# Seven-product block matmuls in another order, sums in place, three convolution tiles, a later norm product

## The chip, the cores and the metric

One core of a Trainium2 chip runs the kernel. The metric is the device time of one execution in microseconds (us). The median of 3 timed runs of the kernel before is 1835.4 us (1834.36 to 1836.99). TensorE (PE) does matmuls into PSUM, VectorE (DVE), ScalarE (ACT) and GpSimd (POOL) do elementwise work, SyncE (SP) issues the DMA transfers.

## The reference, cut to what matters

One layer of a hybrid decoder on x of 1024 tokens by 1024 channels, in float32:

```python
h = rms_norm(x, g_pre)
proj = h @ w_in            # q,k,v,z_a | u,v_s,z_s | z_m, xBC, dt | 3 x 1024 gates
y_att = sliding_window_attention(q, k, v, sinks, rel_bias) * silu(z_a)
y_sg  = chunked_spatial_gate(u, v_s, ...) * silu(z_s)       # u * (tril(W) LN(v_s) + b)
y_ssm = ssd_mixer(z_m, xbc, dt, ...)   # conv of 4 taps + silu on xbc, chunked scan over 8 chunks
                                       # x 4 groups, * silu(z_m), RMS norm per group
merged = sum(sigmoid(gate_i) * (y_i @ w_br_i))              # three branches
out = x + rms_norm(merged @ w_out, g_post)
```

## The kernel before, in words

Each float32 operand of a big matmul is split into a high and a low part (`hi`, `lo`), and three matmuls (hi*hi, hi*lo, lo*hi) stand for one product. The order of TensorE's instructions is written out by hand in the whole kernel; in the pair stage (below), up to its last chunk, that of the other engines and of SP's queue is too. Every engine works its own instructions strictly in that order.

**Stages.** Input norm and first projections (to 350 us), attention with more projections beside it (to 429), then the **pair stage** (429 to 1365), then the three branch matmuls and the output matmul (1365 to the end).

**The pair stage.** 39 units are done, each one projection of 256 output columns (a pair of 128) by 1024 tokens and 1024 channels, as a 2 by 2 block matmul with seven block products in place of eight (class `PairStream`, line 197). The blocks of h are `hB[half of tokens, half of channels]`; three sums of them (`s1`, `s2`, `s4`) are made once. A unit's weights come in two `raw` tiles (3 buffers in turn): the first holds blocks B11 and B12, the second B21 and B22. Four sums of weight blocks, T1 to T4, are made per unit by POOL (`_sum`, line 227), the first in place of B12, the other three in `ts` tiles, of which there are two. `_prepare(q)` (line 236) does the loads and sums for product q and makes its `hi` (ACT, line 257) and, one product later, its `lo` (DVE, line 232). It runs four products ahead of TensorE. The sums therefore stand in POOL's queue between other work, and a sum whose tile is still being read waits, with all that is behind it.

`_step` (line 273) issues one product: 12 matmuls of 128 by 512 columns (lines 293 to 295) into a PSUM tile, of which four are in turn; then `_work()`; then the evacuation, in which ACT or DVE adds the product to running sums in `tp` tiles (lines 309 to 317). A product of a unit is named i = 0 to 6 here. When a block of the result is complete, `evac` gets it: blocks 22, 12, 21, 11 at i = 3, 4, 5, 6.

`_work` (line 264) advances the follow-up jobs by one step per product. At most two jobs are active, as they share two `acc` tiles. A convolution job (`conv`, line 748; the blocks of x, B and C, in units called x units) takes five steps: ACT scales (line 752), DVE does two taps and one tap (line 755), ACT tanh (lines 760, 761), POOL multiplies (line 763) and SP stores. A z job takes two steps (ACT lines 713 and 714, POOL line 716 and a store), a gate job one. The units run as x z x z x g, then three times x z x z x g g, then eight zu units (z of the spatial gate with u) and four g.

**The chunk work** of the scan (`chunk`, line 874) runs beside the products: 32 chunks, one begun every six products (every five in the last group of eight), each advanced by a step per product. Step 0 transposes on TensorE into two PSUM tiles `ps_tr` (lines 884 to 888), which DVE and ACT empty (lines 890, 894 and ACT's `btok`, line 892). Step 4 has DVE's `t1` (line 932), which empties the PSUM tile that the matmuls of step 6 (line 952) use next. Step 13 (12 in the last group) is the **norm product** (line 974), one matmul into `ps_tr`. There are two `ps_tr` tiles; the norm product takes the one that the transposes of the second next chunk used last, and those were issued at step 12 (10 in the last group), so it waits for `btok`.

After the chunks, the spatial gate (lines 1004 to 1062) does eight groups between the remaining products: a load `vg`, POOL (line 1025), DVE (line 1026), TensorE (lines 1035, 1040), DVE. The last four products stand behind it. Then the branch matmuls read their inputs `y` into tiles that lie where those of the pair stage were.

Of the kernel before, what the change touches and what calls it, by code (L numbers as in the profile page):

```python
# [11 lines left out]
F32 = mybir.dt.float32  # L12
F32R = mybir.dt.float32r
AF = mybir.ActivationFunctionType
ALU = mybir.AluOpType
# [4 lines left out]
P = 128  # L20
S = 1024
# [6 lines left out]
NPY = 2  # L28
# [12 lines left out]
def hybrid_kernel(ctx, tc, t, out):  # L41
    nc = tc.nc
    V, A, G, T = nc.vector, nc.scalar, nc.gpsimd, nc.tensor
# [10 lines left out]
    def psum(pool, tag):  # L54
        return pool.tile([P, 512], F32, name="ps_" + tag, tag=tag)
# [141 lines left out]
    class PairStream:  # L197
# [17 lines left out]
                b = self.b.setdefault(u, {})  # L215
                b[f"B{k + 1}1"], b[f"B{k + 1}2"] = r[:, 0:512], r[:, 512:]

        def _sum(self, u, out, x, y, op):
            b = self.b.get(u, {})
            if out in b or u >= len(self.units):  # L220
                return
            if out == "T1":

                b[out] = b[x]
            else:
                b[out] = self.pool.tile([P, 512], F32, name="ts", bufs=2)
            G.tensor_tensor(b[out], b[x], b[y], op=op)  # L227

        def _second(self):
            if self.late is not None:  # L230
# [4 lines left out]
        def _prepare(self, q):  # L235

            u, i = divmod(q, 7)
            self._second()
            if i == 0:
                for k in range(2):  # L240
                    self._load(u, k)
                self._sum(u, "T3", "B22", "B12", ALU.subtract)
                self._sum(u, "T2", "T3", "B11", ALU.add)
            elif i == 1:
                self._sum(u, "T1", "B12", "B11", ALU.subtract)
                self._load(u + 1, 0)
            elif i == 3:
                self._load(u + 1, 1)
            elif i == 4:
                self._sum(u, "T4", "T2", "B21", ALU.subtract)  # L250
            elif i == 6:
                self._sum(u + 1, "T3", "B22", "B12", ALU.subtract)
            src = self.b[u][("B11", "T2", "T1", "T3", "B22", "T4", "B21")[i]]
            if q % 2 == 0:
                self.slot = [wp.tile([P, 1024], F32R, name=n, tag=n, bufs=3) for n in ("whi", "wlo")]
            hi, lo = (x[:, q % 2 * 512:q % 2 * 512 + 512] for x in self.slot)
            A.copy(hi, src)  # L257
            self.late = lo, src, hi
            self.ops[q] = hi, lo
            if i == 6:  # L260
                del self.b[u]

        def _work(self):

            self.waiting, self.fresh = self.waiting + self.fresh, []
            for _ in range(2 if len(self.waiting) > 3 else 1):
                while self.waiting and len(self.active) < 2 and (len(self.begun) < 2 or self.begun[-2] not in self.active):
                    self.active.append(self.waiting.pop(0))
                    self.begun.append(self.active[-1])
                for job in list(self.active):  # L270
                    if next(job, None) is None:
                        self.active.remove(job)

        def _step(self):
            n = 7 * len(self.units)
            if self.done >= n:
                return None
            while self.prepared < min(n, self.done + 1 + self.AHEAD):
                self._prepare(self.prepared)
                self.prepared += 1  # L280
            if self.prepared == self.done + 1:
                self._second()
            u, i = divmod(self.done, 7)
            hi, lo = self.ops.pop(self.done)
            o = psum(ps_ax, "ax") if self.done % 4 == 3 else psum(ps_mm, "mm")
            self.done += 1
            if i == 0:
                self.t = {}
            t = self.t
            for kt in range(4):  # L290
                ks = slice(kt * P, (kt + 1) * P)
                h0, h1 = (self.lhs(i, part, kt) for part in range(2))
                T.matmul(o, lhsT=hi[:, ks], rhs=h0, start=kt == 0, stop=False)  # L293
                T.matmul(o, lhsT=hi[:, ks], rhs=h1, start=False, stop=False)  # L294
                T.matmul(o, lhsT=lo[:, ks], rhs=h0, start=False, stop=kt == 3)  # L295

            def tmp(name):

                t[name] = self.pool.tile([P, 516], F32, name="tp", bufs=8)
                return t[name][:, 4:]  # L300

            def block(b, name, op=ALU.add):
                d = t[name][:, 4:]
                V.tensor_tensor(d, d, o, op=op)  # L304
                self.units[u][1](b, t[name])

            self._work()
            if i == 0:
                A.copy(tmp("s1"), o)
            elif i == 1:  # L310
                t["u2"] = self.pool.tile([P, 512], F32, name="tu", bufs=1)
                V.tensor_tensor(t["u2"], t["s1"][:, 4:], o, op=ALU.add)
            elif i == 2:
                V.tensor_tensor(tmp("u4"), t["u2"], o, op=ALU.add)
            elif i == 3:
                V.tensor_tensor(tmp("c22"), t["u4"][:, 4:], o, op=ALU.add)
                V.tensor_tensor(tmp("u3"), t["u2"], o, op=ALU.add)
                self.units[u][1](22, t["c22"])
            elif i == 4:
                block(12, "u4")  # L320
            elif i == 5:
                block(21, "u3", ALU.subtract)
            else:
                block(11, "s1")
            return 2.8

        def run(self, n):
# [45 lines left out]
    if True:  # L373

        with tc.tile_pool(name="xp", bufs=1) as xp:
# [96 lines left out]
            n = NB * 32  # L472
# [206 lines left out]
    sop = es7.enter_context(tc.tile_pool(name="sop", bufs=1, side="right", reuse_waits="tile"))  # L679
    s2, s1, s4 = ([sop.tile([P, 4, 512], F32R, name=f"S{i}{part}") for part in range(2)] for i in (2, 1, 4))  # L680

    blocks = [hB[0, 0], s2, s1, hB[1, 0], s4, hB[1, 1], hB[0, 1]]

    ep = es7.enter_context(tc.tile_pool(name="ep", bufs=1, side="right", reuse_waits="tile"))
    pst = PairStream(ep, lambda i, part, kt: blocks[i][part][:, kt, :])
# [6 lines left out]
    def gate_pair(n):  # L692
        def tanh(b, d):
            A.activation(d, d, AF.Tanh, scale=0.5)
            i, half = NGATE + 2 * n + b % 10 - 1, b // 10 - 1
            nc.sync.dma_start(out=gate_dr[i, :, half * 512:(half + 1) * 512], in_=d)
            yield from ()

        def evac(b, d):
            pst.fresh.append(tanh(b, d[:, 4:]))  # L700
        return [t["w_gp"][n][k] for k in range(2)], evac

# [6 lines left out]

    def z_pair(g, n):  # L710
        def silu(b, d):
            th = ap.tile([P, 512], F32, name="acc", bufs=2)
            A.activation(th, d, AF.Tanh, scale=0.5)
            A.activation(th, th, AF.Identity, bias=one)
            yield 1
            G.tensor_tensor(d, th, d, op=ALU.mult)
            store(z_dr, g, b // 10 - 1, 2 * n + b % 10 - 1, d)

        def evac(b, d):
            pst.fresh.append(silu(b, d[:, 4:]))  # L720
        return [t["w_zm"][2 * g + n][k] for k in range(2)], evac

    def zu_pair(g):
        us = {}

        def silu(half, d, u):
            th = ap.tile([P, 512], F32, name="acc", bufs=2)
            A.activation(th, d, AF.Tanh, scale=0.5)
            yield 1
            V.scalar_tensor_tensor(d, th, 1.0, d, op0=ALU.add, op1=ALU.mult)  # L730
            yield 1
            V.scalar_tensor_tensor(d, u, 0.5, d, op0=ALU.mult, op1=ALU.mult)
            nc.sync.dma_start(out=uz_dr[g, :, half * 512:(half + 1) * 512], in_=d)

        def evac(b, d):

            half, d = b // 10 - 1, d[:, 4:]
            if b in (12, 22):
                us[half] = d
            else:  # L740
                pst.fresh.append(silu(half, d, us.pop(half)))
        return [t["w_zu"][g][k] for k in range(2)], evac

    def conv_pair(g, n):

        held = {}

        def conv(half, k, d):
            ti = g * 4 + 2 * n + k if n < 2 else 16 + 4 * k + g
            body = d[:, 4:]  # L750
            acc = ap.tile([P, 512], F32, name="acc", bufs=2)
            A.activation(acc, body, AF.Identity, scale=wcv[:, ti, 3:4], bias=bcv[:, ti:ti + 1])  # L752
            yield 1
            for tap in range(3):
# [11 lines left out]
            else:  # L766
                store(bc_dr, g, half, k, body)

        def evac(b, d):
            half, k = b // 10 - 1, b % 10 - 1  # L770
            if half == 1:
                held[k] = d
                return
            V.memset(d[:, 1:4], 0.0)
            d1 = held.pop(k)
            V.tensor_copy(d1[:, 1:4], d[:, 513:516])
            pst.fresh += [conv(0, k, d), conv(1, k, d1)]

        return [t["w_xbc"][3 * g + n][k] for k in range(2)], evac

# [49 lines left out]
    with tc.tile_pool(name="mp", bufs=1, reuse_waits="tile") as mp, tc.manual_schedule(  # L830
# [43 lines left out]
        def chunk(n):  # L874
# [95 lines left out]
            yield  # L970
            yield
            yield
            pn = psum(ps_tr, "tr")
            T.matmul(pn[:, 0:1], lhsT=ss, rhs=one, start=True, stop=True)
            A.copy(ssum[:, n:n + 1], pn[:, 0:1])
# [91 lines left out]
    spare = {}  # L1067
# [68 lines left out]
    for n in (9, 10, 11):  # L1136
        spare[n] = slot(n)
    pz.tile([P, 384], F32, name="pz_pad")
    for n in (2, 3):
        raws[n] = raw_tile(n)  # L1140
    for n in range(NPY, 9):
        spare[n] = slot(n)
    merged.extend(pz.tile([P, S], F32, name=f"mg{i}") for i in range(8))
    for n in range(NPY, 8):
        ys[n] = load_y(n)
    for un in range(4):
# [128 lines left out]
```

## Time and profile before

| what | us |
|---|---|
| median of 3 runs | 1835.4 |
| the profiled execution: its own time, its span | 1831.66, 1830.0 |
| TensorE busy | 1750.5 (96%) |
| VectorE busy | 1287.7 (70%) |
| ScalarE busy | 844.2 (46%) |
| GpSimd busy | 850.8 (46%) |
| DMA | 243.28 MB, mean 133 GB/s |

A matmul's busy time counts its passage through the array too, so TensorE shows as busy where it merely goes from one matmul to the next; what it loses shows as gaps (the table of waits) and as stretches in which the granted clock is half. A wait is put down to whatever came last.

### The profile page before, as it was taken

The numbers are of one execution on the slowest core, as the hardware profiler recorded it, in microseconds if no ns is written. First come the engines' busy times: TensorE is split into PE (matmuls) and PEld (weight loads), VectorE is DVE, ScalarE is ACT, GpSimd is POOL, SyncE is SP. The second block draws the span as 40 slices with busy tenths as digits, with TensorE's granted clock in tenths as the row PEclk, the third lists the DMA queues.
The fourth block names the chain that finished last, engine by engine and source line by source line (L and its number), as shares of the span: only waits on it lengthen the run. The fifth ranks groups of instructions, "written<-read, shape, count | busy, mean of one in ns | idle before, by whom it ended". The sixth has DMA issues, their size and how long they took to land. (4 is left out here: it accounts for less than half of the span.)

```text
span 1830.0 us, 25921 instructions
## 1 busy us (share of the span) xinstructions
PE 1750.5 (96%) x9181; PEld 1474.7 (81%) x9181; DVE 1287.7 (70%) x1781; ACT 844.2 (46%) x1883; POOL 850.8 (46%) x761
## 2 busy tenths in 40 slices
PE   7999999998999989998999899999988999999998
PEld 6988888897887777877777778887776888888898
DVE  5466667758888888898889878987885284444424
ACT  5245555534555766576666666552233122111221
POOL 1015666665655877587667766667424050000000
PEclk9999999999999999999999999999998999999999
DMA  7221111122334546454644555544767353533204
GB/s 227 67 73 47 47 58 47 58 67 73 115 93 150 173 138 205 126 155 150 202 139 144 155 190 161 157 147 126 236 233 261 127 195 106 181 121 98 81 24 162
DMA packets 165377, 243.28 MB, mean 133 GB/s; under 512 B 13152, under 2 KB 105600, under 8 KB 165120
## 3 DMA queue, kind: packets, MB, share of 16 engines
q1 hardware_dynamic: 165248, 241.63, 41.6%
q8 instruction: 73, 1.20, 0.3%
q14 instruction: 56, 0.46, 0.1%
HBM read 177.99 MB, written 63.59 MB: 132 GB/s over the span
## 5 line engine op out<-in xcount | busy, mean ns | idle before, releaser
L116 PE MATMUL ps_mm<-y,whi 128*128 128x512 f32 x512 | 200.4, 391 | 9.7 <-ACT y L1094 9.7
L117 PE MATMUL ps_mm<-y,whi 128*128 128x512 f32 x512 | 200.3, 391 | 1.4 <-DVE y L1095 1.4
L293 PE MATMUL ps_mm<-h,whi 128*128 128x512 f32 x468 | 194.1, 415 | 7.4 <-ACT vst L354 3.4
L118 PE MATMUL ps_mm<-y,wlo 128*128 128x512 f32 x512 | 199.9, 390 | 0.0
L227 POOL TENSOR_TENSOR ts<-ts,raw 128x512 f32<-128x512 f32 x78 | 123.6, 1585 | 152.9 <-DVE wlo L232 150.3
L98 ACT CAST whi<-raw 128x1024 fp32r<-128x1024 f32 (+1 forms) x69 | 71.5, 1038 | 251.6 <-PE ps_mm L117 224.4
L294 PE MATMUL ps_mm<-h,whi 128*128 128x512 f32 x468 | 185.4, 396 | 0.0
L295 PE MATMUL ps_mm<-h,wlo 128*128 128x512 f32 x468 | 185.2, 396 | 0.0
L232 DVE TENSOR_TENSOR wlo<-raw,whi 128x512 fp32r<-128x512 f32 x156 | 176.4, 1131 | 8.6 <-ACT whi L257 8.4
L89 POOL TENSOR_TENSOR rso<-rso,mhalf_row 128x1 f32<-128x1 f32 x8 | 4.4, 553 | 323.1 <-DVE rso L88 323.1
L755 DVE SCALAR_TENSOR_TENSOR acc<-tp,wcv,acc 128x512 f32<-128x512 f32 x144 | 146.7, 1046 | 2.5 <-ACT acc L752 0.8
L293 PE MATMUL ps_mm<-S,whi 128*128 128x512 f32 x352 | 143.8, 408 | 0.3 <-DVE tp L304 0.3
L295 PE MATMUL ps_mm<-S,wlo 128*128 128x512 f32 x352 | 137.7, 391 | 0.6 <-DVE wlo L232 0.6
L294 PE MATMUL ps_mm<-S,whi 128*128 128x512 f32 x352 | 137.6, 391 | 0.0
L116 PE MATMUL ps_mm<-h,whi 128*128 128x512 f32 x304 | 121.0, 398 | 2.0 <-ACT vst L354 2.0
L257 ACT CAST whi<-raw 128x512 fp32r<-128x512 f32 x156 | 94.6, 612 | 60.9 <-POOL raw L227 45.9
L116 PEld LDWEIGHTS ps_mm<-y,whi 128*128 128x128 f32 x512 | 96.6, 189 | 30.6 <-ACT y L1094 10.5
L1118 DVE SCALAR_TENSOR_TENSOR tm<-gld,ps_mm 128x512 f32<-128x512 f32 x48 | 32.9, 686 | 122.3 <-PE ps_mm L118 122.3
L118 PE MATMUL ps_mm<-h,wlo 128*128 128x512 f32 x304 | 118.6, 390 | 0.0
L117 PE MATMUL ps_mm<-h,whi 128*128 128x512 f32 x304 | 118.6, 390 | 0.0
L117 PEld LDWEIGHTS ps_mm<-y,whi 128*128 128x128 f32 x512 | 96.6, 189 | 22.8 <-DVE y L1095 3.0
L293 PEld LDWEIGHTS ps_mm<-h,whi 128*128 128x128 f32 x468 | 89.7, 192 | 29.6 <-issue 4.1
(242 smaller groups left out, 4945.1 us busy)
## 6 DMA issues: line engine op xcount, KB each, us to landing
seg<-acs_dr SPq DMA_DIRECT2D x64, 256.0 KB, 3.9
raw<-in_w_br_dram SPq DMA_DIRECT2D x32, 512.0 KB, 4.5
yraw<-y_dr SPq DMA_DIRECT2D x32, 512.0 KB, 5.0
gld<-gate_dr SPq DMA_DIRECT2D x32, 512.0 KB, 3.5
raw<-in_w_xbc_dram SPq DMA_DIRECT2D x24, 512.0 KB, 4.0
raw<-in_w_gp_dram SPq DMA_DIRECT2D x22, 512.0 KB, 4.3
gate_dr<-tp SPq DMA_DIRECT2D x44, 256.0 KB, 3.3
raw<-in_w_zm_dram SPq DMA_DIRECT2D x16, 512.0 KB, 3.6
```

The costliest lines, as they stand in the source:

```text
L98: A.copy(hi, raw)
L116: T.matmul(ps, lhsT=whi[:, ks], rhs=rhs(0, kt, half), start=kt == 0, stop=False)
L117: T.matmul(ps, lhsT=whi[:, ks], rhs=rhs(1, kt, half), start=False, stop=False)
L118: T.matmul(ps, lhsT=wlo[:, ks], rhs=rhs(0, kt, half), start=False, stop=kt == KT - 1)
L227: G.tensor_tensor(b[out], b[x], b[y], op=op)
L232: V.tensor_tensor(lo, src, hi.bitcast(F32), op=ALU.subtract)
L257: A.copy(hi, src)
L293: T.matmul(o, lhsT=hi[:, ks], rhs=h0, start=kt == 0, stop=False)
L294: T.matmul(o, lhsT=hi[:, ks], rhs=h1, start=False, stop=False)
L295: T.matmul(o, lhsT=lo[:, ks], rhs=h0, start=False, stop=kt == 3)
L755: V.scalar_tensor_tensor(acc, d[:, 1 + tap:513 + tap], wcv[:, ti, tap:tap + 1], acc, op0=ALU.mult, op1=ALU.add)
L1118: V.scalar_tensor_tensor(tm, gt[0][:, fs], 1.0, ps, op0=ALU.add, op1=ALU.mult)
```

## The change

- The seven products of a unit stand in another order: B11, B21, T2, T1, T3, B22, T4 (before: B11, T2, T1, T3, B22, T4, B21). Blocks 11, 12, 22, 21 are complete at i = 1, 5, 5, 6, so four follow-up jobs come at those. The running sums are made in fewer tiles: `tu` goes, and sums are updated in place. Per unit there are, as before, one ACT copy and seven DVE adds, four `tp` tiles and two small copies of the convolution's edge.
- T2 is written in place of B11 and T3 in place of B12, T1 and T4 in the two `ts` tiles. All four are subtractions. T2 and T3 are issued at `_prepare` step 1, T1 at step 0, T4 at step 4. The next unit's weights are loaded at steps 3 and 5 (before: 1 and 3).
- Three `acc` tiles and up to three active jobs.
- The norm product stands two products later (chunk step 15, in the last group 14).
- The tiles of the branch stage lie in another order over those of the pair stage.

```diff
@@ -215,16 +215,12 @@
...
-        def _sum(self, u, out, x, y, op):
-            b = self.b.get(u, {})
-            if out in b or u >= len(self.units):
+        def _sum(self, u, out, x, y, place=None):
+            if u >= len(self.units) or out in self.b[u]:
                 return
-            if out == "T1":
-
-                b[out] = b[x]
-            else:
-                b[out] = self.pool.tile([P, 512], F32, name="ts", bufs=2)
-            G.tensor_tensor(b[out], b[x], b[y], op=op)
+            b = self.b[u]
+            b[out] = b[place] if place else self.pool.tile([P, 512], F32, name="ts", bufs=2)
+            G.tensor_tensor(b[out], b[x], b[y], op=ALU.subtract)
@@ -239,18 +235,18 @@
...
                     self._load(u, k)
-                self._sum(u, "T3", "B22", "B12", ALU.subtract)
-                self._sum(u, "T2", "T3", "B11", ALU.add)
+                self._sum(u, "T1", "B12", "B11")
             elif i == 1:
-                self._sum(u, "T1", "B12", "B11", ALU.subtract)
+
+                self._sum(u, "T2", "B22", "T1", "B11")
+                self._sum(u, "T3", "B22", "B12", "B12")
+            elif i == 3:
                 self._load(u + 1, 0)
-            elif i == 3:
+            elif i == 4:
+                self._sum(u, "T4", "T2", "B21")
+            elif i == 5:
                 self._load(u + 1, 1)
-            elif i == 4:
-                self._sum(u, "T4", "T2", "B21", ALU.subtract)
-            elif i == 6:
-                self._sum(u + 1, "T3", "B22", "B12", ALU.subtract)
-            src = self.b[u][("B11", "T2", "T1", "T3", "B22", "T4", "B21")[i]]
+            src = self.b[u][("B11", "B21", "T2", "T1", "T3", "B22", "T4")[i]]
             if q % 2 == 0:
@@ -264,7 +260,7 @@
...
             for _ in range(2 if len(self.waiting) > 3 else 1):
-                while self.waiting and len(self.active) < 2 and (len(self.begun) < 2 or self.begun[-2] not in self.active):
+                while self.waiting and len(self.active) < 3 and (len(self.begun) < 3 or self.begun[-3] not in self.active):
                     self.active.append(self.waiting.pop(0))
@@ -299,29 +295,32 @@
...
-            def block(b, name, op=ALU.add):
-                d = t[name][:, 4:]
-                V.tensor_tensor(d, d, o, op=op)
-                self.units[u][1](b, t[name])
-
             self._work()
+
+            def sum_(name, x):
+                V.tensor_tensor(tmp(name), t[x][:, 4:], o, op=ALU.add)
+
+            evac = self.units[u][1]
             if i == 0:
-                A.copy(tmp("s1"), o)
+                A.copy(tmp("s"), o)
             elif i == 1:
-                t["u2"] = self.pool.tile([P, 512], F32, name="tu", bufs=1)
-                V.tensor_tensor(t["u2"], t["s1"][:, 4:], o, op=ALU.add)
+                sum_("c11", "s")
+
+                evac(11, t["c11"], t["s"])
             elif i == 2:
-                V.tensor_tensor(tmp("u4"), t["u2"], o, op=ALU.add)
+                V.tensor_tensor(t["s"][:, 4:], t["s"][:, 4:], o, op=ALU.add)
             elif i == 3:
-                V.tensor_tensor(tmp("c22"), t["u4"][:, 4:], o, op=ALU.add)
-                V.tensor_tensor(tmp("u3"), t["u2"], o, op=ALU.add)
-                self.units[u][1](22, t["c22"])
+                sum_("u4", "s")
             elif i == 4:
-                block(12, "u4")
+                sum_("c22", "u4")
+                V.tensor_tensor(t["s"][:, 4:], t["s"][:, 4:], o, op=ALU.add)
             elif i == 5:
-                block(21, "u3", ALU.subtract)
+                V.tensor_tensor(t["u4"][:, 4:], t["u4"][:, 4:], o, op=ALU.add)
+                evac(12, t["u4"], t["c22"])
+                evac(22, t["c22"], None)
             else:
-                block(11, "s1")
+                V.tensor_tensor(t["s"][:, 4:], t["s"][:, 4:], o, op=ALU.subtract)
+                evac(21, t["s"], None)
             return 2.8
@@ -679,7 +678,7 @@
...
-    blocks = [hB[0, 0], s2, s1, hB[1, 0], s4, hB[1, 1], hB[0, 1]]
+    blocks = [hB[0, 0], hB[0, 1], s2, s1, hB[1, 0], s4, hB[1, 1]]
@@ -696,7 +695,7 @@
...
-        def evac(b, d):
+        def evac(b, d, after):
             pst.fresh.append(tanh(b, d[:, 4:]))
@@ -709,14 +708,14 @@
...
         def silu(b, d):
-            th = ap.tile([P, 512], F32, name="acc", bufs=2)
+            th = ap.tile([P, 512], F32, name="acc", bufs=3)
             A.activation(th, d, AF.Tanh, scale=0.5)
...
-        def evac(b, d):
+        def evac(b, d, after):
             pst.fresh.append(silu(b, d[:, 4:]))
@@ -724,7 +723,7 @@
...
         def silu(half, d, u):
-            th = ap.tile([P, 512], F32, name="acc", bufs=2)
+            th = ap.tile([P, 512], F32, name="acc", bufs=3)
             A.activation(th, d, AF.Tanh, scale=0.5)
@@ -732,23 +731,22 @@
...
-        def evac(b, d):
+        def evac(b, d, after):
             half, d = b // 10 - 1, d[:, 4:]
-            if b in (12, 22):
+            if half in us:
+                z, u = (d, us[half]) if b % 10 == 1 else (us[half], d)
+                pst.fresh.append(silu(half, z, u))
+            else:
                 us[half] = d
-            else:
-                pst.fresh.append(silu(half, d, us.pop(half)))
         return [t["w_zu"][g][k] for k in range(2)], evac
...
     def conv_pair(g, n):
-
-        held = {}
...
             body = d[:, 4:]
-            acc = ap.tile([P, 512], F32, name="acc", bufs=2)
+            acc = ap.tile([P, 512], F32, name="acc", bufs=3)
             A.activation(acc, body, AF.Identity, scale=wcv[:, ti, 3:4], bias=bcv[:, ti:ti + 1])
@@ -766,15 +764,12 @@
...
-        def evac(b, d):
+        def evac(b, d, after):
             half, k = b // 10 - 1, b % 10 - 1
-            if half == 1:
-                held[k] = d
-                return
-            V.memset(d[:, 1:4], 0.0)
-            d1 = held.pop(k)
-            V.tensor_copy(d1[:, 1:4], d[:, 513:516])
-            pst.fresh += [conv(0, k, d), conv(1, k, d1)]
+            if half == 0:
+                V.memset(d[:, 1:4], 0.0)
+                V.tensor_copy(after[:, 1:4], d[:, 513:516])
+            pst.fresh.append(conv(half, k, d))
@@ -970,6 +965,8 @@
...
             yield
+            yield
+            yield
             pn = psum(ps_tr, "tr")
@@ -1136,11 +1133,14 @@
...
     pz.tile([P, 384], F32, name="pz_pad")
+    for n in (5, 6, 7, 8):
+        spare[n] = slot(n)
+    merged.extend(pz.tile([P, S], F32, name=f"mg{i}") for i in range(4))
     for n in (2, 3):
         raws[n] = raw_tile(n)
-    for n in range(NPY, 9):
+    for n in (2, 3, 4):
         spare[n] = slot(n)
-    merged.extend(pz.tile([P, S], F32, name=f"mg{i}") for i in range(8))
+    merged.extend(pz.tile([P, S], F32, name=f"mg{i}") for i in range(4, 8))
     for n in range(NPY, 8):
```

## Rows read from the trace of the kernel before

**Rows 1.** The page's parts 1: span, and busy time of each engine.

```profile
span 1830.0 us, 25921 instructions
...
PE 1750.5 (96%) x9181; PEld 1474.7 (81%) x9181; DVE 1287.7 (70%) x1781; ACT 844.2 (46%) x1883; POOL 850.8 (46%) x761
```

**Rows 2.** Stretches: from:to, length, busy of each engine (instructions), clock, DMA.

```profile
600.00:776.00 176.00, 165.99 (x847) 134.02 (x846) 153.04 (x199) 116.53 (x260) 125.09 (x93) 0.97 0.53 160
...
1110.00:1254.00 144.00, 143.85 (x768) 116.83 (x767) 125.35 (x158) 75.70 (x187) 91.62 (x68) 1.00 0.49 147
1264.00:1363.00 99.00, 92.47 (x468) 77.60 (x468) 82.16 (x106) 24.56 (x44) 43.73 (x31) 0.98 0.61 199
```

**Rows 3.** Waits of TensorE, whole span: total us, times, longest.

```profile
PE ps_tr L974 <- ACT btok L892: 14.2, 7, 4.0
PE ps_ac L952 <- DVE ea L932: 12.2, 11, 3.9
...
PE ps_mm L116 <- ACT y L1094: 9.7, 2, 9.3
PE ps_mm L293 <- ACT vst L354: 3.4, 1, 3.4
PE ps_mm L293 <- DVE tu L312: 3.2, 1, 3.2
...
PE ps_tr L974 <- POOL tp L716: 1.2, 2, 0.6
```

**Rows 4.** Ten microseconds behind each of TensorE's four long gaps: columns of rows 2.

```profile
605.10:615.10 10.00, 10.00 (x50) 8.51 (x51) 9.93 (x15) 6.66 (x17) 9.92 (x7) 0.75 0.40 104
657.50:667.50 10.00, 10.00 (x38) 8.13 (x39) 8.55 (x12) 8.51 (x20) 10.00 (x7) 0.83 0.40 116
833.80:843.80 10.00, 9.97 (x35) 8.17 (x36) 8.95 (x12) 8.54 (x20) 10.00 (x8) 0.75 0.41 128
1010.60:1020.60 10.00, 9.96 (x33) 8.12 (x34) 8.59 (x12) 8.65 (x20) 10.00 (x8) 0.71 0.43 129
```

**Rows 5.** Timeline 649 to 658: start, us, engine, line, tiles [idle before <- releaser].

```profile
649.35 1.29 POOL L227 TENSOR_TENSOR ts<-ts,raw 128x512 f32<-128x512 f32 x1 [5.55 <-DVE wlo L232]
...
650.19 0.60 PE L888 MATMUL ps_tr<-ident,xch 128*128 128x128 f32 x4
...
650.59 3.01 POOL L763 TENSOR_TENSOR tp<-tp,acc 128x512 f32<-128x512 f32 x2
...
652.38 0.63 ACT L713 ACTIVATE acc<-tp 128x512 f32<-128x512 f32 x1 [4.15 <-POOL tp L763]
...
655.55 0.69 DVE L312 TENSOR_TENSOR tu<-tp,ps_ax 128x512 f32<-128x512 f32 x1 [4.36 <-ACT tp L309]
...
657.50 0.35 PE L974 MATMUL ps_tr<-mhalf_row,ssy 128*128 128x1 f32 x2 [3.93 <-ACT btok L892]
```

**Rows 6.** Waits of POOL, then of SP's queue, 429 to 1370.

```profile
POOL ts L227 <- DVE wlo L232: 150.3, 42, 9.1
...
SPq L213 <- DVE wlo L232: 201.7, 49, 9.5
```

**Rows 7.** Timeline of TensorE: the chunk matmuls of step 6, two of three.

```profile
605.09 1.12 PE L952 MATMUL ps_ac<-seg,xdt 128*64 128x128 f32 x8 [3.87 <-DVE ea L932]
...
958.58 1.09 PE L952 MATMUL ps_ac<-seg,xdt 128*64 128x128 f32 x16 [1.53 <-DVE ea L932]
```

**Rows 8.** DVE on tile tp: count, ns least/median/most, first and last start.

```profile
L755 DVE SCALAR_TENSOR_TENSOR acc<-tp,wcv,acc x144: 737/752/1789, 448.6 to 1051.6; 128x512 f32<-128x512 f32 x144
L304 DVE TENSOR_TENSOR tp<-tp,ps_mm x77: 670/680/690, 444.7 to 1243.8; 128x512 f32<-128x512 f32 x77
```

**Rows 9.** Timeline: last norm product, first spatial-gate group on DVE and TensorE.

```profile
1254.52 0.28 PE L974 MATMUL ps_tr<-mhalf_row,ssy 128*128 128x1 f32 x2
...
1267.95 1.29 DVE L1026 TENSOR_TENSOR vg<-vg,rsv 128x1024 f32<-128x1024 f32 x1 [6.86 <-POOL vg L1025]
...
1271.10 0.38 PE L1035 MATMUL ps_tr<-sgw,ones 128*128 128x128 f32 x2
```

## The prediction

> **What bounds the kernel now.** I read the page's first part, then busy time by stage, then TensorE's waits, and then single stalls in the timeline of all engines. The reader is to see four things.
>
> TensorE is the bound: it is busy 1750.5 of 1830.0 us [rows 1]. The change leaves its matmuls as they are (39 units of 7 products of 12 matmuls), so all that can move is what TensorE loses in gaps and at a low clock.
>
> The loss lies where chunks of the groups 0 to 2 run. Between 600 and 776 TensorE has 10.0 us without work, while in the last group, 1110 to 1254, it has 0.15 us in 144 [rows 2]. The same code runs in both; the difference is three convolution units in seven, and that the chunks there are one step shorter and five apart.
>
> By TensorE's waits [rows 3] the norm product L974 costs 14.2 + 1.2 = 15.4 us in nine gaps, and L952, the chunk matmuls of step 6, 12.2 us in eleven. What else stands in that table belongs to other places: 9.7 us at the start of the branches, 3.4 at the first product, 3.2 in the spatial gate.
>
> A gap costs more than itself. Behind the four long gaps the granted clock of the next 10 us is 0.75, 0.83, 0.75 and 0.71 [rows 4], a mixture of the full level, 2.4 GHz, and the half one, 1.2 GHz, which it fell to as TensorE stood still. Work lost in each is 10 us times what is missing to 1: 2.5 (behind L952 at 605), 1.7, 2.5 and 2.9 us (behind L974 at 657, 834 and 1011).
>
> The timeline of 649 to 658 shows one knot [rows 5]. POOL waits 5.55 us for a `lo` of DVE, since a sum (T4) wants the `ts` tile that this `lo` still reads. Behind it stands the convolution's multiply L763. ACT waits 4.15 us for that with L713, as there are two `acc` tiles only. Behind L713 stands the copy L309, for which DVE waits 4.36 us, and behind that on DVE and ACT the emptying of `ps_tr`. So TensorE, which issued the transposes at 650.19 and one product later wants the norm product, stands for 3.93 us. POOL's wait for `lo` occurs 42 times, 150.3 us in all [rows 6], about once a unit.
>
> **The norm product two products later.** A product takes 2.76 us: between the last norm product at 1254.52 and the spatial gate's first matmul at 1271.10 there are six of them, 16.58 / 6 [rows 9]. The norm product's tile was used by transposes issued one product before; now it is three before (four in the last group), 5.5 us more. The longest wait is 4.0 us [rows 3], shorter than that, so all nine gaps go even if nothing else became earlier: -15.4 us, and with them 1.7 + 2.5 + 2.9 = 7.1 us of low clock [rows 4]. Together -22.5 us. What is behind it: `ssum`'s copy on ACT, and POOL's next write of `ssy`, which has one product of room left in the first groups and none in the last one; there POOL may wait up to a product for TensorE. POOL is busy 91.62 of 144 us there [rows 2], which covers it; uncovered it would be 8 times 2.76, 22 us, of POOL's time and not TensorE's.
>
> **Sums in place, products in another order.** No sum is added or dropped, and DVE and ACT empty the same count of products. T4 now finds its `ts` tile long free. T2 instead writes over B11 and waits for the `lo` of B11 that is issued in the same step: one wait a unit as before, at another product. Of the three sums before whose `hi` came one product later (T2, T1, T4) one is left, T2. What stood behind the waiting sum, the multiplies of the previous unit's convolutions, now mostly stands ahead of it: blocks 12 and 22 multiply at i = 3 of the next unit, T2 comes at i = 4, block 21 behind it. The second load of weights goes to step 5; it must wait for the `lo` of T3 of the same step. Its first use is three products later, as before, 8.3 us. SP waited for a `lo` 49 times, 4.1 us each, 9.5 at most [rows 6]; the first load (now step 3) finds its tile free, which takes about half of these away, from 0 to 201.7 us of a queue's time, none of which TensorE waited for by rows 3. I take 0 for it; if cover ended, POOL and ACT would wait behind the load, not TensorE, which is four products away.
>
> **Third convolution tile.** It ends ACT's wait for POOL (L713) in the knot, as the tile wanted is now that of the third last job, done two products earlier. The L952 gaps that come right behind such a knot go with it: 3.87 us at 605, and the same place in the next two groups, down to 1.53 us at 959 [rows 7], three in all and some 7 us, with 2.5 us of low clock behind the first: -9.5 us. Bounds for L952: nothing, and all of 12.2 + 2.5 = 14.7 us. The other eight gaps (about 5 us together) follow DVE's own bursts; I leave them.
>
> Against this stands a burst. Blocks 12 and 22 arrive together at i = 5 and 21 one later; with three jobs active DVE gets four taps in each of two neighbouring products. Alone a tap takes 752 ns [rows 8]: 8 x 0.75 = 6.0 us, with two `lo` (some 0.7 each), one add (0.68) and the chunk's share (about 1.6) 9.7 us, against 5.5 us of products. DVE falls some 4 us behind, and step 6 tolerates two products, 5.5 us. In some places it will not do: +4 us, between 0 and the third rival.
>
> The trace shows a tap between 737 and 1789 ns and an add that reads PSUM between 670 and 690 ns [rows 8]. The Trainium skill, "GPSIMD Engine Reference", section "Specifications", has a rule for it: POOL's way to SBUF is shared with VectorE, and DVE instructions with two SBUF inputs contend. By it the taps that meet T2 and T3 on POOL take the long time, and the burst overruns the room; that result is the third rival.
>
> **The rest.** The spatial gate starts two products nearer to the last norm product: of the 26 products left there are 24, of the 3 before its first mix 2. From the norm product at 1254.52 to its DVE's end at 1267.95 + 1.29 is 14.7 us [rows 9]; five products take 13.8. So +0.9 us; from -3.2 (the wait on `tu`, which is gone [rows 3]) to +5.5 (both products). The branches start behind the last product by a chain of evacuation, store and load of 9.7 us [rows 3]; the input tiles still lie over blocks that are read early in the last unit, and I take 0, between -9.7 and +4. The first product's wait (3.4) hangs on ACT's splits in front, which stay: 0.
>
> **Sum.** -22.5 - 9.5 + 4 + 0.9 = -27.1 us. The profiled execution took 1831.66 us, so 1804.6; it lies 3.7 us under the median of 1835.4, to which the same difference gives 1808 us.
>
> **Rivals.**
>
> *Only the norm product gains.* POOL's one wait a unit is still there, behind it multiplies and sums, and DVE, whose 153.04 of 176 us [rows 2] become 92% when 10 us go, stays late; then TensorE, no longer held at L974, arrives earlier at L952 and pays half of the gain back: -22.5 + 11 = -11.5, 1824 us. For it: both gaps have one cause. Against: the last group runs DVE at 87% without a gap [rows 2].
>
> *All goes.* No gap is left in the stage and the gate's wait goes too: -22.5 - 14.7 - 3.2, and a part of the branches' wait, say -4: -44, 1791 us. For it: the last group. Against: the bursts.
>
> *DVE's burst takes over; slower.* Nine convolution units run beside chunks. If three of the eight taps and the `lo` beside them meet POOL, which is busy 125 of 176 us [rows 2], three times (1.79 - 0.75) = 3.1 us join the 4 of lag: 7 us, over the 5.5 that L952 tolerates. It decides where the burst falls on chunk steps 4 to 6. At its full price, the 3.87 us of 605 at each of the nine, and the L952 gaps kept: +35 - 22.5 = +12, 1848 us. For it: taps up to 1789 ns. Against: the jobs before came in bursts of four taps too, and the step that matters meets one burst in three or so.
>
> *It doesn't do what it says.* T2's wait for `lo` and the load behind it make a new knot as long as the old one: the norm product is free, but all evacuations move back alike and gaps appear at the products instead; within 0.2% of before.
>
> **How the numbers follow.** Chances: the forecast 0.56, with its own range 1797 to 1819 (the spatial gate and the branches from -5 to +5, bursts from 0 to 10); only the norm product 0.19; all goes 0.10; burst 0.10; no effect 0.05. The range from 1795 to 1829 leaves out about 0.2: the burst, no effect, and part of the best case. About 0.2%, 3.7 us, is what a measurement of this kernel can tell from no change. Faster by more: 0.56 + 0.19 + 0.10 less a little of the second, 0.84; slower 0.10; the same 0.06.
>
> **What would show it.** Right: no row of L974 over 0.5 us among TensorE's waits; clock 1.00 in all windows between 610 and 1250; POOL's waits for `lo` well under 150 us; ACT's wait at L713 for POOL gone. Burst: L952 waiting for `t1` with taps over 1.5 us ahead of it. Wrong: gaps in front of products (L293) between 450 and 1250, or the span of the spatial gate longer by more than 5 us.

## The result, and the profile after

The changed kernel takes 1814.64 us (median of 4 runs, 1813.3 to 1815.05), beside 1836.2 us for the kernel before in the same series: a ratio of 0.9882, 95% interval [0.9865, 0.9899], 21.6 us less. Forecast were 27 us less. The profiled execution has a span of 1811.6 us against 1830.0 [rows 1].

The page's first part after. TensorE's busy time and every other one stay nearly as they were; what went is time without work:

```profile
span 1811.6 us, 26027 instructions
...
PE 1744.7 (96%) x9181; PEld 1470.6 (81%) x9181; DVE 1271.1 (70%) x1781; ACT 842.0 (46%) x1883; POOL 843.7 (47%) x761
```

Stretches after (columns of rows 2). The chunks of the first group lose 6.0 us in 170 where they lost 10.0 in 176; the last group runs without a gap, as before:

```profile
600.00:770.00 170.00, 164.05 (x854) 132.58 (x853) 150.26 (x198) 114.28 (x256) 125.00 (x92) 1.00 0.52 163
...
1094.00:1238.00 144.00, 144.00 (x758) 117.33 (x756) 120.37 (x158) 75.72 (x185) 86.15 (x68) 1.00 0.50 154
1250.00:1346.00 96.00, 89.32 (x456) 74.29 (x455) 75.12 (x102) 24.08 (x42) 39.78 (x29) 1.00 0.69 227
```

Waits of TensorE while chunks run, after (columns of rows 3; L947 is what was L952, the chunk matmuls of step 6; L930 is the state matmul of step 4; L289 and L291 are the products' own matmuls):

```profile
PE ps_ac L930 <- POOL xde L901: 6.4, 3, 2.2
PE ps_mm L289 <- DVE tp L301: 3.2, 2, 2.1
PE ps_ax L289 <- DVE tp L301: 2.3, 1, 2.3
PE ps_mm L291 <- DVE wlo L228: 1.8, 2, 0.9
PE ps_ac L947 <- DVE ea L927: 1.6, 4, 0.4
PE ps_ax L291 <- DVE wlo L228: 0.9, 1, 0.9
```

The norm product (15.4 us in [rows 3]) has no row any more and step 6 keeps 1.6 of 12.2 us. New are 6.4 us in which TensorE waits for POOL's `xde`, and 3.2 + 2.3 + 1.8 + 0.9 = 8.2 us in which a product waits for DVE: the add that empties its PSUM tile, or a `lo`. Five of these gaps are longer than 2 us (2.0 to 2.3). Behind them the clock of the next 10 us, the third column from the end, is:

```profile
636.40:646.40 10.00, 9.53 (x54) 7.41 (x55) 5.98 (x7) 8.70 (x19) 9.92 (x9) 1.00 0.51 141
680.90:690.90 10.00, 8.69 (x51) 6.74 (x52) 8.93 (x13) 7.24 (x16) 5.66 (x5) 1.00 0.24 72
808.20:818.20 10.00, 9.72 (x55) 7.55 (x56) 5.95 (x7) 8.68 (x19) 9.92 (x9) 1.00 0.49 142
852.70:862.70 10.00, 9.07 (x44) 6.88 (x45) 8.92 (x13) 7.25 (x16) 5.66 (x5) 0.83 0.23 70
981.10:991.10 10.00, 9.94 (x50) 7.31 (x50) 5.91 (x7) 8.64 (x19) 9.92 (x10) 0.83 0.50 139
```

That is 1.7 + 1.7 = 3.4 us of work lost to the half clock, where [rows 4] had 9.6. So far this looks like the forecast: old gaps gone, a burst of DVE's in their place, larger than thought. But gaps in front of products were named as a sign of being wrong, and the experiments show that the sum came out of other parts.

### The profile page after: what moved, and what is told of

It is laid out like the page before. It is cut to its first block, busy times and chain, and to the rows that moved or that the text cites. A ratio compares the mean times of both kernels' runs of the same rounds, so it can differ in the third digit from the quotient of the medians.

```text
span 1811.6 us, 26027 instructions
## 1 busy us (share of the span) xinstructions
PE 1744.7 (96%) x9181; PEld 1470.6 (81%) x9181; DVE 1271.1 (70%) x1781; ACT 842.0 (46%) x1883; POOL 843.7 (47%) x761
## 5 line engine op out<-in xcount | busy, mean ns | idle before, releaser
L228 DVE TENSOR_TENSOR wlo<-raw,whi 128x512 fp32r<-128x512 f32 x195 | 193.6, 994 | 24.8 <-ACT whi L253 21.3
L289 PE MATMUL ps_mm<-h,whi 128*128 128x512 f32 x468 | 192.4, 411 | 3.7 <-ACT vst L353 3.7
L291 PE MATMUL ps_mm<-h,wlo 128*128 128x512 f32 x468 | 183.0, 391 | 0.0
L253 ACT CAST whi<-raw 128x512 fp32r<-128x512 f32 x195 | 118.8, 613 | 93.2 <-POOL raw L223 72.3
L289 PE MATMUL ps_mm<-S,whi 128*128 128x512 f32 x352 | 142.1, 404 | 4.6 <-DVE tp L301 3.5
L753 DVE SCALAR_TENSOR_TENSOR acc<-tp,wcv,acc 128x512 f32<-128x512 f32 x144 | 145.1, 1027 | 1.7
L291 PE MATMUL ps_mm<-S,wlo 128*128 128x512 f32 x352 | 137.5, 391 | 1.8 <-DVE wlo L228 1.8
L223 POOL TENSOR_TENSOR ts<-raw 128x512 f32<-128x512 f32 x78 | 123.9, 1589 | 17.0 <-DVE wlo L228 12.4
L118 PEld LDWEIGHTS ps_mm<-y,wlo 128*128 128x128 f32 x512 | 97.1, 190 | 20.2
```

Of the source, the lines that this page charges most:

```text
L118: T.matmul(ps, lhsT=wlo[:, ks], rhs=rhs(0, kt, half), start=False, stop=kt == KT - 1)
L223: G.tensor_tensor(b[out], b[x], b[y], op=ALU.subtract)
L228: V.tensor_tensor(lo, src, hi.bitcast(F32), op=ALU.subtract)
L753: V.scalar_tensor_tensor(acc, d[:, 1 + tap:513 + tap], wcv[:, ti, tap:tap + 1], acc, op0=ALU.mult, op1=ALU.add)
```

## The experiments

All ratios are to the kernel before in the same series, with 95% intervals; us are the ratio's difference from 1, times 1834. Line numbers shift by a few in each kernel.

| kernel | order and sums | acc tiles, jobs | norm product | ratio | us |
|---|---|---|---|---|---|
| norm_only | before | 2, 2 | later | 1.0002 [0.9993, 1.0011] | 0 |
| order_only | new | 2, 2 | step 13 | 0.9883 [0.9867, 0.9898] | -21 |
| acc_two | new | 2, 2 | later | 0.9807 [0.9793, 0.9820] | -35 |
| three_tiles_two_jobs | new | 3, 2 | later | 0.9820 [0.9803, 0.9837] | -33 |
| norm_back | new | 3, 3 | step 13 | 0.9953 [0.9941, 0.9966] | -9 |
| the changed kernel | new | 3, 3 | later | 0.9882 [0.9865, 0.9899] | -22 |

**norm_only.** The kernel before with one edit:

```diff
+            yield
+            yield
             pn = psum(ps_tr, "tr")
```

> The kernel before with the norm product two products later and nothing else. Forecast's theory: all 15.4 us of gaps at L974 and the 7.1 us of low clock behind three of them go, -22.5 us. Rival: TensorE only arrives earlier at the matmuls of chunk step 6, whose gaps grow by about half of that: -11 us, with 20 us or more of waits on t1 where there were 12.2.

Not a microsecond: 1834.26 against 1833.83 us. TensorE's longest waits with chunks running:

```profile
PE ps_ac L952 <- DVE ea L932: 27.8, 12, 5.5
PE ps_tr L884 <- DMA bcch<-bc_dr: 4.1, 3, 1.9
PE ps_ac L935 <- POOL xde L906: 0.8, 3, 0.3
```

The 15.4 us at the norm product are gone and L952 has 27.8 in place of 12.2, 15.6 more. The clock goes with them: behind the three new long gaps it reads 0.73, 0.75, 0.77, so 7.5 us, where the norm product's had cost 7.1.

```profile
697.70:707.70 10.00, 9.96 (x48) 8.46 (x49) 9.12 (x13) 7.46 (x16) 4.39 (x3) 0.73 0.33 107
875.70:885.70 10.00, 9.96 (x49) 8.44 (x50) 9.14 (x13) 7.46 (x16) 4.39 (x3) 0.75 0.30 109
1053.60:1063.60 10.00, 10.00 (x50) 8.50 (x51) 9.28 (x14) 7.54 (x16) 4.47 (x3) 0.77 0.32 109
```

The rival had half of it given back; all is. DVE and ACT are as late as before (ACT waits 27.3 us at L713, where it waited 26.9), and TensorE meets that at its next need.

**norm_back, acc_two, order_only.** The changed kernel with the norm product back at step 13; with two tiles and two jobs; with both.

```diff
-            th = ap.tile([P, 512], F32, name="acc", bufs=3)
+            th = ap.tile([P, 512], F32, name="acc", bufs=2)      # all three acc tiles
-    while self.waiting and len(self.active) < 3 and (... self.begun[-3] not in self.active):
+    while self.waiting and len(self.active) < 2 and (... self.begun[-2] not in self.active):
```

> The changed kernel with the norm product back at step 13. If the new order and the third tile undo the knot by themselves, ACT's btok is in time, no gap over 1 us comes back at the norm product and the time stays within 5 us of the changed kernel. Rival: DVE's burst makes btok as late as before, gaps of 3 to 4 us come back at some six norm products: +15 to +22 us, no better than the kernel before.

> The changed kernel with two acc tiles and two active jobs. If the third tile makes the burst in which DVE falls behind (8 taps in two products), the new gaps, products waiting for an add and the state matmul waiting for POOL's xde, go, and the kernel is 5 to 15 us faster than the changed one. Rival: two tiles tie the knot again at ACT's wait for POOL, gaps at t1 come back to some 10 us: 5 to 10 us slower than the changed one.

> The changed kernel with two acc tiles and the norm product at step 13: the new product order, sums in place and layout alone. If the sum that waits for the lo of B11 is as good as the one that waited for the lo of T3, it is level with the kernel before, within 5 us. Rival: the multiplies now stand ahead of the waiting sum, the knot is gone, and it is 10 to 15 us faster than before; or the new order by itself bunches the jobs and it is slower by 5 or more.

The new order alone gains 21 us; the expectation had none, its rival 10 to 15. With it, the later norm product is worth 14 us (order_only to acc_two), and 13 beside three jobs (norm_back to the changed kernel); in order_only its waits were 11.9 us and step 6 had but 3.2:

```profile
PE ps_tr L969 <- ACT btok L887: 11.9, 12, 2.6
PE ps_ac L947 <- DVE ea L927: 3.2, 6, 0.7
```

In norm_back the gaps at the norm product come back too, 17.4 us of them, up to 2.7 us long. It is 13 us slower than the changed kernel: its expectation fails, and its rival, at +15 to +22, is nearly met. And the third tile with the third job costs: without them 1798.02 us, the fastest kernel here that leaves nothing out, ahead of both the one before and the changed one. Its whole list of TensorE's waits with chunks running is one row:

```profile
PE ps_ac L947 <- DVE ea L927: 10.1, 9, 1.3
```

**three_tiles_two_jobs.** The changed kernel with `len(self.active) < 2` and all else as it is.

> The changed kernel with three acc tiles but two active jobs. If the loss of the third tile is the burst of three jobs' taps on DVE, it is level with two tiles, -36 us against before, within 4. Rival: the loss lies in the tile itself (ACT starts scalings earlier, ahead of more urgent work): level with the changed kernel, -22.

Level with two tiles. With two jobs the third tile neither helps nor harms; the third active job costs 11 to 14 us.

**one_start, add_first, add_first_two.** Two ways to soften three jobs' burst: begin at most one job per advance; or issue a product's add ahead of `_work` (in the changed kernel, and in acc_two).

```diff
-    while self.waiting and len(self.active) < 3 and (...):
+    if self.waiting and len(self.active) < 3 and (...):
```

```diff
-            self._work()
+            self.waiting, self.fresh = self.waiting + self.fresh, []
             ...
                 evac(21, t["s"], None)
+            new, self.fresh = self.fresh, []
+            self._work()
+            self.fresh = new
```

> The changed kernel, three tiles and three jobs, but at most one job is begun per advance, so that the taps of blocks 12, 22 and 21 come as 2, 3, 3, 1 in four products and not as 4, 4, 1. If the burst is what costs, the products' waits for an add and for lo go, 10 to 16 us faster than the changed kernel. Rival: three jobs at a time are late whatever their order: within 4 us of the changed kernel.

> The changed kernel (three tiles, three jobs) with each product's add issued ahead of the jobs' step, not behind it; the jobs begin at the same products as before. If the third job costs because a product's add and the next lo stand behind the eight taps in DVE's queue, the products' waits (8.1 us) go and it is 6 to 12 us faster than the changed kernel. Rival: POOL's chain behind DVE (y, xde, the waiting sum) is what is late; the products' waits go, the state matmul's grow, within 4 us of the changed kernel.

> The same with two tiles and two jobs. If the adds' place matters wherever taps come in a burst, 3 to 8 us faster than two tiles alone, so -39 to -44 against before. Rival: with two jobs no product waits for an add, so nothing is to be had, within 3 us; taps that come later make t1 late, and up to 5 us are lost.

Beginning one job at a time: 0.9869 [0.9851, 0.9887], not told apart from the changed kernel. The products' waits fell to 2.0 us, as the expectation has it, but step 6 waits 8.1 where it waited 1.6. Adds first: 0.9905 [0.9890, 0.9919], level as well; products still wait 6.9 us, now for a `lo` alone, and the state matmul 6.5 as before. So the order of DVE's work within a step does not make the cost. With two jobs, adds first lose 9 us: 0.9856 [0.9839, 0.9873]. Its gaps sum to as much as in acc_two, but there are three long ones instead of nine short (last section).

**no_inplace_sums.** The changed kernel without T2 and T3 on POOL.

```diff
-            G.tensor_tensor(b[out], b[x], b[y], op=ALU.subtract)
+            if place is None:
+                G.tensor_tensor(b[out], b[x], b[y], op=ALU.subtract)
```

> The changed kernel without its sums T2 and T3: B11 and B12 are used as they are, so 78 of POOL's 156 sums of weight blocks, and the waits for the lo of B11 in front of them, are left out. If the third job costs because its taps run beside POOL and take up to 1.79 us, slow taps become few, the products' waits for an add go and the time falls to that of two tiles, -36 us against before. Rival: the burst by itself is what is late; the taps become shorter, but 5 us or more of products waiting for an add and for lo stay, and the gain on the changed kernel is under 8 us, from the state matmul's wait for xde.

0.9772 [0.9749, 0.9794]: 20 us faster than the changed kernel, though three jobs are active. The time falls to that of two tiles and below, and the products' waits are gone, but not for the expected reason: taps take 989 ns on average for 1027, and 32 of 144 are over 1.5 us where 40 were, so slow ones did not become few. The rival fails. And the burst is still there. DVE's taps of one burst and the add behind it, first in the changed kernel, then here; last, acc_two at the same place, where the taps come as two, one, two, one with other work between them (its first three are shown):

```profile
667.16 4.02 DVE L753 SCALAR_TENSOR_TENSOR acc<-tp,wcv,acc 128x512 f32<-128x512 f32 x4
...
673.63 6.59 DVE L753 SCALAR_TENSOR_TENSOR acc<-tp,wcv,acc 128x512 f32<-128x512 f32 x4
680.14 0.67 DVE L301 TENSOR_TENSOR tp<-tp,ps_mm 128x512 f32<-128x512 f32 x1
```

```profile
661.17 2.98 DVE L754 SCALAR_TENSOR_TENSOR acc<-tp,wcv,acc 128x512 f32<-128x512 f32 x4
...
666.60 6.63 DVE L754 SCALAR_TENSOR_TENSOR acc<-tp,wcv,acc 128x512 f32<-128x512 f32 x4
673.15 0.68 DVE L302 TENSOR_TENSOR tp<-tp,ps_mm 128x512 f32<-128x512 f32 x1
```

```profile
664.68 2.56 DVE L753 SCALAR_TENSOR_TENSOR acc<-tp,wcv,acc 128x512 f32<-128x512 f32 x2
...
669.69 1.78 DVE L753 SCALAR_TENSOR_TENSOR acc<-tp,wcv,acc 128x512 f32<-128x512 f32 x1
671.40 0.67 DVE L301 TENSOR_TENSOR tp<-tp,ps_mm 128x512 f32<-128x512 f32 x1
```

Eight taps take 10.6 us in the changed kernel and 9.6 without the sums; yet without them the only wait left on TensorE with chunks running is 3.9 us at step 6. What else the sums take away is DVE's waiting for others. In the changed kernel DVE, late as it is, stands still for ACT's `hi` and for POOL:

```profile
DVE wlo L228 <- ACT whi L253: 21.3, 8, 3.7
DVE st L938 <- POOL st L934: 18.0, 10, 2.8
```

Without T2 and T3 these are 1.6 and 6.5 us; with two jobs (acc_two) 1.7 and 3.3. These waits fit a ring: DVE's burst delays the `lo` of B11, T2 on POOL waits for it with POOL's queue behind, ACT's `hi` of T2 or T3 waits for POOL, and DVE waits for that `hi`.

Shown is that taking away either the third job or the sums takes the cost away, while the eight taps stay in the second case. The ring is a reading, and its middle links do not set the changed kernel apart. ACT's `hi` waits 55.3 us for POOL there, 47.5 in acc_two and 59.2 in three_tiles_two_jobs, which is as fast. The sums in place wait for a `lo` 43.2 us in the changed kernel and 76.4 in acc_two, here in this order:

```profile
POOL raw L223 <- issue: 49.9, 15, 4.5
POOL raw L223 <- DVE wlo L228: 43.2, 12, 8.7
```

```profile
POOL raw L223 <- DVE wlo L228: 76.4, 19, 8.7
...
POOL raw L223 <- issue: 6.4, 2, 4.5
```

"Issue" is idle time for which the profile names nobody; with it the two kernels have 93 and 83 us of idle time before these sums. How much of the 20 us is the sums' wait and how much their time on POOL is not separated, and no kernel without the sums was tried with two jobs. As acc_two has only 10.1 us of waits left there and the full clock, some 10 us is the most that leaving them out could gain in it, by estimate; so at least about half of the 20 hangs on the third job.

**t4_place, t4_place_norm.** What in the new order is it? The kernel before with the one waiting sum freed, T4 over T2's tile; and that with the later norm product.

```diff
+            elif out == "T4":
+                b[out] = b["T2"]
             else:
                 b[out] = self.pool.tile([P, 512], F32, name="ts", bufs=2)
```

> The kernel before with T4 written over T2's tile, which is free two products earlier, so that POOL's sum no longer waits for the lo of T3 with the multiplies behind it; order, tiles and norm product as before. If that waiting sum ties the knot, POOL's 150 us of waits for lo fall under 60, ACT's wait at L713 goes and the kernel gains what the new order alone gained: -18 to -25 us. Rival: the gain of the new order is that blocks are complete at other products; then within 5 us of before.

> The same with the norm product two products later as well. If TensorE's waits at the norm product are what is left once the knot is cut, -30 to -38 us against before, as the changed kernel with two acc tiles. Rival: they move to the matmuls of step 6 again, within 5 us of the kernel without the later norm product.

0.9941 [0.9926, 0.9956] and 0.9937 [0.9921, 0.9953]: 11 us for the freed sum, nothing for the norm product on top. POOL's waits for `lo` fell as expected, to 59.1 us, and ACT's wait at L713 is gone, as is DVE's for the copy behind it. Before they were:

```profile
ACT acc L713 <- POOL tp L763: 26.9, 8, 4.7
```

```profile
DVE tu L312 <- ACT tp L309: 34.8, 8, 4.4
```

The 11 us are half of order_only's gain, and short of the 18 to 25 us expected. TensorE's long gaps are gone with the knot, but of 28.5 us of waits 22.8 stay, in shorter pieces:

```profile
PE ps_ac L954 <- DVE ea L934: 13.6, 8, 2.4
PE ps_tr L976 <- ACT btok L894: 6.7, 6, 2.1
PE ps_tr L976 <- POOL tp L718: 2.5, 3, 1.3
```

With the later norm product its 9.2 us of these go, and step 6 has 20.0 us for 13.6, with gaps of up to 3.7. The other half of the new order's gain must lie in what t4_place lacks: blocks complete at i = 1, 5, 5, 6, sums in place, loads at steps 3 and 5, the layout. Which of these was not tried.

**late_step6.** acc_two with step 6 one product later in the first three groups, against its one wait; the norm product stays at step 15.

```diff
             if g < 3:
                 yield
+                yield
...
-            yield
+            if g == 3:
+                yield
             pn = psum(ps_tr, "tr")
```

> The changed kernel with two acc tiles and two jobs, and the chunk matmuls of step 6 one product later in the first three groups (the norm product stays at step 15). If TensorE's nine waits of about 1.2 us on t1 there (10.1 us) only come of DVE being late by less than a product, they go: -8 to -11 us against two tiles alone, -44 to -47 against before. Rival: they move to the next place where TensorE needs DVE or POOL, within 3 us of two tiles alone.

A miss, and not only by size: 0.9894 [0.9876, 0.9912], 16 us slower than acc_two. Step 6 waits 1.0 us, but the state matmul now waits 10.1 us for POOL's `xde` and products 4.5 us for a `lo`. The edit brings a wait of its own. There is one `xdt` tile: DVE fills it at a chunk's step 0, POOL makes `xde` from it, and the matmuls of step 6 read it. Step 0 of the next chunk is six products later, so with step 6 moved it comes ahead of these reads, and DVE stands still for them:

```profile
DVE xdt L889 <- PE ps_ac L948: 17.1, 9, 3.1
```

acc_two has no such row. That this makes `xde` late fits, but no kernel with a second `xdt` tile was tried. So the run does not tell whether the nine short waits could be had by themselves.

## Why the prediction was right, and where it was not

The time lay in the range, some 5 us from the forecast's 27; the division was wrong, and that the sum came out so near is luck.

- *What bounds the kernel, and the knot*: right as far as it goes. With the waiting sum freed alone, ACT's wait at L713 and DVE's for the copy behind it are gone, the long gaps too, and 11 us with them. But 22.8 us of shorter gaps stay, so the knot was not the cause of them all.
- *The norm product, -22.5 us*: this is the step that failed. All nine gaps went, "even if nothing else became earlier", and so they did in norm_only; but nothing was gained: step 6 took 15.6 us of gaps in place of 15.4 and 7.5 us of low clock in place of 7.1, as TensorE's gap was not the norm product's own but DVE's and ACT's lateness met there. The first rival had this mechanism, at half its size. Only with the new order is the later norm product worth 13 to 14 us; with the knot cut by t4_place it is worth nothing.
- *Order and sums in place, 0*: -21 us. The prediction saw that the multiplies now mostly stand ahead of the waiting sum, but put nothing on it and credited the end of the knot to the third tile. Freeing a sum alone gives 11 us (t4_place); where the rest comes from is open.
- *Third tile, -9.5, and its burst, +4*: together -5.5; measured +11 to +14. Most of the knot at L713 is gone without a third tile (7.5 us of that wait are left in acc_two, 26.9 were there). The burst was seen and put at a third of its price. What the sum leaves out is that DVE, late as it is, also stands still for POOL's state and ACT's next `hi`: 39.3 us in the changed kernel, 5.0 in acc_two.
- *The rule of shared ports*: the Trainium skill, "GPSIMD Engine Reference", section "Specifications", has VectorE instructions with two SBUF inputs contend with POOL. The trace agrees: the changed kernel's taps take 734 to 1785 ns; POOL was at work for at least two thirds of the time of each of the 40 over 1.5 us, and for a fifth, on average, of that of the 96 under 0.8. But the mean tap is 1027 ns there and 1199 in the faster acc_two, so slow taps don't make the third job's cost, and the rival built on them fails in its reason.
- *The spatial gate, +0.9*: right. From the last norm product at 1240.96 to the first gate matmul at 1255.27 are 14.3 us, with gaps of 0.31 us before that and 0.68 before the first mix. The wait on `tu` left with the tile.
- *The branches, 0*: right within its bounds. The long gap, a few us into the stage, is 7.7 us for 9.3:

```profile
1359.93 0.79 PE L116 MATMUL ps_mm<-y,whi 128*128 128x512 f32 x1 [7.70 <-ACT y L1091]
```

This matmul starts 19.7 us earlier than the one at 1379.63 before, and the program ends 18.4 us earlier, so 1.3 us were lost behind it.

The parts as measured, one after the other: -21.5 for the order, -13.9 for the norm product on top of it, +13.8 for the third tile and job, together -21.6. As forecast: 0, -22.5 and -9.5 + 4, with the gate's +0.9 together -27.1. Errors of 21, 9 and 19 us nearly cancelled.

Of what was said to show the forecast right, three things came true and could not tell these apart: no row of L974, 64 us of POOL's waits for a `lo` in place of 150, 2.7 us of ACT's wait at L713 in place of 26.9. The fourth failed: the clock of 1.00 in all windows, which reads 0.83 in two. And a sign of being wrong came, the 8.2 us of gaps in front of products.

## What to carry to other kernels

A gap on the bound engine names the place where it met somebody's lateness. Moving that place (the norm product) gained nothing while the late engines were as late; look first for what makes them late, here in part one sum that waits at the head of an in-order queue. More jobs in flight are not faster by themselves: two were 11 to 14 us faster than three. And parts that were never measured alone can be wrong by 20 us each under a right sum.

## What the runs showed of the hardware

How gaps are cut up can matter as much as their sum. acc_two and add_first_two both lose some 10 us in gaps with chunks running: nine of at most 1.3 us, 10.1 in all, and three of 3.4 to 3.5 us, 10.3 in all. In the first the granted clock stays at 1.00 between 600 and 1094:

```profile
600.00:1094.00 494.00, 483.90 (x2521) 392.86 (x2520) 460.88 (x577) 334.97 (x760) 370.58 (x268) 1.00 0.55 167
```

In the second it falls to the half level at each gap, and reads over the next 10 us:

```profile
642.80:652.80 10.00, 10.00 (x47) 8.43 (x48) 8.39 (x13) 6.38 (x15) 6.45 (x6) 0.71 0.57 182
813.20:823.20 10.00, 10.00 (x47) 8.40 (x48) 8.28 (x12) 6.38 (x15) 6.45 (x6) 0.70 0.61 181
983.70:993.70 10.00, 10.00 (x46) 8.45 (x47) 8.25 (x12) 6.38 (x15) 6.44 (x6) 0.69 0.60 180
```

2.9 + 3.0 + 3.1 = 9.0 us lost, as much as lies between the two kernels (1798.0 and 1807.0). Of the changed kernel's five gaps of 2.0 to 2.3 us above, two cost clock and three did not.
